# DoRA forward on one core: stores on ScalarE's ring, chunks in pairs, and part of block 0 loaded by GpSimd

## The chip, the core and the metric

The kernel runs on one core of a Trainium2 chip. The time is device microseconds of that core; the kernel before took 164.54 us, the median of 9 runs (164.23 to 164.89). A profiled execution gives the page and the trace that are read here.

## The reference

A weight matrix is adapted by a product of rank 16, its columns are normalised and scaled, and a batch of 32,768 rows of 256 numbers is multiplied by it.

```python
W_adapted = W + scale * (lora_A @ lora_B)                 # 256 x 256
W_norm = np.sqrt(np.sum(W_adapted ** 2, axis=0, keepdims=True) + 1e-8)
W_final = W_adapted / W_norm * m
y = x.reshape(-1, 256) @ W_final                          # 32768 x 256, float32
```

`x` and `y` have 33.55 MB each. All else is small: `W` has 256 KB.

## The kernel before

The rows of `x` are cut into 8 blocks (`NBLK`) of 4096 rows, 4 MB each. A block lies in SBUF as 128 partitions by 32 rows (`DJ`) of 256 numbers, so that a partition's share is 32 KB that follow each other in DRAM. There are five such buffers (`x_bufs`, L63). A block is worked on in 8 chunks (`CH`) of 4 rows per partition (`J`), 64 chunks in all.

SyncE issues all large transfers on one ring. It loads `W` and then the first five blocks (`load_x`, L106 to L121). After that its loop (L124 to L131) waits until block b is done, issues its store (L126), waits until the store of block b-1 has landed and issues the load of the block that takes that buffer. ScalarE's ring carries only the three small loads of `lora_A`, `lora_B` and `m` (L115 to L119).

The prologue makes the final weights in bf16 (`w_final`): four small products on TensorE (L213 to L229), the arithmetic on VectorE (L158 to L182) and the square root on ScalarE (L195).

After that each chunk goes through five engines. GpSimd waits for the block's load at its first chunk and rounds the chunk to bf16 (L151, `xb`, four buffers). TensorE turns it by four transposes of pairs of bf16 that are read as fp32 (`turned`, L243, into one of four PSUM tiles `xt_ps`). VectorE copies that tile to SBUF (L185, `xt`, four buffers). TensorE multiplies it with `w_final` in eight matmuls (`product`, L254, into one of two PSUM tiles `y_ps`). ScalarE copies the result over the chunk of `x` that it came from (L202), and after the eighth chunk of a block it drains and raises `done` (L206), for which SyncE waits.

The order on TensorE is written out by hand: a loop over the 8 blocks (L268), whose body turns chunk 0 and then, for each chunk, turns the next chunk of the same block before it multiplies this one. `take` (L234) waits for a semaphore and takes one from it, which makes the body the same in each round. `head_slot` places the head of the loop among the instructions. At the end of the program SyncE waits for the last five stores (L280).

Of the kernel before, what the change touches and what calls it, by code (L numbers as in the profile page):

```python
# [11 lines left out]
def kernel(  # L12
# [10 lines left out]
    nc = tc.nc  # L23
    P = 128
    FP32 = mybir.dt.float32
    BF16 = mybir.dt.bfloat16
# [3 lines left out]
    x_flat = x.flatten_outer_dims()  # L30
    out_flat = out.flatten_outer_dims()
    N, IN = x_flat.shape
    OUT = W.shape[1]
    R = lora_A.shape[1]
    KC = IN // P
    J = 4
    DJ = 32
    BLK = DJ * P
    NBLK = N // BLK
# [3 lines left out]
    XBUFS = 5  # L43
    CH = DJ // J
    NCH = NBLK * CH
    NXB = 4
    NXT = 4
    F4 = J * P

    PE = mybir.EngineType.PE  # L50

# [5 lines left out]
    def sb(name, shape, dtype):  # L57
        return ctx.enter_context(nc.sbuf_tensor(name, shape, dtype))

    def ps(name, shape, dtype):  # L60
        return ctx.enter_context(nc.psum_tensor(name, shape, dtype))

    x_bufs = [sb(f"x_sb{k}", [P, DJ, IN], FP32) for k in range(XBUFS)]  # L63
    xb_bufs = [sb(f"xb{k}", [P, J, IN], BF16) for k in range(NXB)]
    xt_bufs = [sb(f"xt{k}", [P, F4, KC], BF16) for k in range(NXT)]
    w_nat = sb("w_nat", [P, KC, OUT], FP32)
    a_nat = sb("a_nat", [P, KC, R], FP32)
    b_nat = sb("b_nat", [R, OUT], FP32)
# [13 lines left out]
    m_all = sb("m_all", [P, OUT], FP32)  # L82
    w_final = sb("w_final", [P, KC, OUT], BF16)

    xt_ps = [ps(f"xt_ps{k}", [P, F4], FP32) for k in range(4)]
    y_ps = [ps(f"y_ps{k}", [P, J, OUT], FP32) for k in range(2)]

    aT_ps = y_ps[0][0:R, 0, :]
# [2 lines left out]
    mb_ps = y_ps[1][:, 2, :]  # L91


    late = [nc.alloc_semaphore(f"store{b}") for b in range(NBLK - XBUFS, NBLK)]
    sems = {f"store{b}": late[b - NBLK + XBUFS] for b in range(NBLK - XBUFS, NBLK)}

    def sem(name):
        if name not in sems:
            sems[name] = tc.alloc_semaphore(name)
        return sems[name]  # L100

    def rows(dram, b):
        return dram[b * BLK : (b + 1) * BLK].rearrange("(p j) k -> p j k", p=P)


    def load_x(b):  # L106
        nc.sync.dma_start(out=x_bufs[b % XBUFS][:], in_=rows(x_flat, b)).then_inc(
            sem(f"load{b}"), 16
        )


    nc.sync.dma_start(
        out=w_nat[:], in_=W.rearrange("(p t) o -> p t o", t=KC)
    ).then_inc(sem("load_w"), 16)
    nc.scalar.dma_start(  # L115
        out=a_nat[:], in_=lora_A.rearrange("(p t) r -> p t r", t=KC)
    ).then_inc(sem("load_a"), 16)
    nc.scalar.dma_start(out=b_nat[:], in_=lora_B).then_inc(sem("load_b"), 16)
    nc.scalar.dma_start(out=m_row[:], in_=m[None, :]).then_inc(sem("load_m"), 16)  # L119
    for b in range(XBUFS):  # L120
        load_x(b)  # L121


    for b in range(NBLK):  # L124
        nc.sync.wait_ge(sem("done"), b + 1)
        nc.sync.dma_start(out=rows(out_flat, b), in_=x_bufs[b % XBUFS][:]).then_inc(  # L126
            sem(f"store{b}"), 16
        )
        if b >= 1 and b - 1 + XBUFS < NBLK:
            nc.sync.wait_ge(sem(f"store{b - 1}"), 16)  # L130
            load_x(b - 1 + XBUFS)  # L131


    nc.gpsimd.memset(zeros[:], 0.0).then_inc(sem("pool"), 1)
# [2 lines left out]
        out=identity[:],  # L137
        in_=zeros[:],
# [3 lines left out]
        pattern=[[-1, P]],  # L142
        channel_multiplier=1,
    ).then_inc(sem("ident"), 1)
    for g in range(NCH):
        b, c = divmod(g, CH)
        if c == 0:
            nc.gpsimd.wait_ge(sem(f"load{b}"), 16)
        if g >= NXB:
            nc.gpsimd.wait_ge(sem("turned"), g - NXB + 1)  # L150
        nc.gpsimd.tensor_copy(  # L151
            out=xb_bufs[g % NXB][:],
            in_=x_bufs[b % XBUFS][:, c * J : (c + 1) * J, :],
        ).then_inc(sem("rounded"), 1)


    dv = sem("dve")
# [9 lines left out]
        out=wa[:], in0=ab_ps, scalar=float(scale), in1=w_nat[:], op0=ALU.mult, op1=ALU.add  # L167
# [6 lines left out]
    for t in range(KC):  # L174
        i = nc.vector.tensor_mul(out=wam[:, t], in0=wa[:, t], in1=m_all[:])  # L175
# [4 lines left out]
    for t in range(KC):  # L180
        i = nc.vector.tensor_mul(out=w_final[:, t], in0=wam[:, t], in1=rnorm[:])  # L181
    i.then_inc(dv, 1)  # L182
    for g in range(NCH):
        nc.vector.wait_ge(sem("turned"), g + 1)
        nc.vector.tensor_copy(  # L185
            out=xt_bufs[g % NXT][:].rearrange("p r t -> p (r t)").bitcast(FP32),
            in_=xt_ps[g % 4][:],
        ).then_inc(sem("copied"), 1)


# [5 lines left out]
        out=norm[:], in_=n2_ps, func=AF.Sqrt, bias=eps_col[:]  # L196
    ).then_inc(sem("act"), 1)
    for g in range(NCH):
        b, c = divmod(g, CH)
        nc.scalar.wait_ge(sem("product"), g + 1)  # L200

        nc.scalar.copy(  # L202
            out=x_bufs[b % XBUFS][:, c * J : (c + 1) * J, :], in_=y_ps[g % 2][:]
        ).then_inc(sem("room"), 1)
        if c == CH - 1:
            nc.scalar.drain().then_inc(sem("done"), 1)  # L206


    pe = sem("pe")
# [2 lines left out]
    for t in range(KC):  # L212
        i = nc.tensor.transpose(aT_ps[:, t * P : (t + 1) * P], a_nat[:, t, :], identity[:])  # L213
    i.then_inc(pe, 1)
    nc.tensor.wait_ge(dv, 2)
    for t in range(KC):
        i = nc.tensor.matmul(  # L217
            ab_ps[:, t, :], aT[:, t * P : (t + 1) * P], b_bf[:], start=True, stop=True
        )
# [3 lines left out]
    for t in range(KC):  # L223
        i = nc.tensor.matmul(  # L224
            n2_ps, ones[:], sq[:, t, :], start=(t == 0), stop=(t == KC - 1)
        )
# [7 lines left out]
    def take(name):  # L234

        nc.tensor.sem_inc(sem(name), -1).wait_op(sem(name), 1, "sem-ge")  # L236

    j_order = []
# [1 line left out]
        j_order.append(a)  # L240
        j_order.append(a + J // 2)

    def turned(c):  # L243
        take("rounded")

        for j in range(J):
            i = nc.tensor.transpose(  # L247
                xt_ps[c % 4][:, j * P : (j + 1) * P],
                xb_bufs[c % NXB][:, j, :].bitcast(FP32),
                identity[:],  # L250
            )
        i.then_inc(sem("turned"), 1)

    def product(c):  # L254
        take("copied")
        take("room")
        for t in range(KC):
            for j in j_order:
                i = nc.tensor.matmul(  # L259
                    y_ps[c % 2][:, j, :],  # L260
                    xt_bufs[c % NXT][:, j * P : (j + 1) * P, t],
                    w_final[:, t, :],
                    start=(t == 0 and (j % (J // 2)) == 0),
                    stop=(t == KC - 1 and (j % (J // 2)) == (J // 2) - 1),
                )
        i.then_inc(sem("product"), 1)

    with nc.Fori(0, NBLK, 1, engines=[PE], head_slot={PE: 0}):  # L268
        turned(0)
        for c in range(CH):  # L270
            if c + 1 < CH:
                turned(c + 1)
            product(c)


    critical.close()
# [40 lines left out]
```

## Time and profile before

| what | value |
|---|---|
| median of 9 runs | 164.54 us (164.23 to 164.89) |
| profiled execution | 164.6 us |
| its span, first to last instruction | 163.3 us |
| busy: TensorE matmuls, ScalarE, GpSimd, VectorE | 100.1, 66.8, 65.4, 49.7 us |
| moved by DMA | 67.45 MB, 413 GB/s over the span |
| read and written in HBM | 33.85 and 33.55 MB |
| loads of `x`: 8 of 4 MB, median from issue to landing | 29.6 us |
| stores: 8 of 4 MB, median from issue to landing | 35.7 us |
| last ScalarE copy begins, last store is issued | 139.66 us, 140.74 us |

The span is counted from the first to the last instruction of the profiled execution; the run's own time is somewhat longer. The page cuts the span into 40 slices of 4.08 us and gives each engine's busy share of a slice in tenths; the row DMA is the mean over the 16 DMA engines. The table of queues gives packets, megabytes and the time of the packets as a share of the 16 engines' span[...]. The waits are ordered by who waited for whom, with the total, the number and the longest in us. The stretches give, between two times, the busy time of each engine with its number of instructions, the granted clock of TensorE, the DMA share and the rate.

### The profile page before, as it was taken

Reading aid. Unit: us, or ns where it says so; the run is one execution under the profiler, and the core shown is the slowest. Engines: PE = TensorE matmul, PEld = TensorE weight load, DVE = VectorE, ACT = ScalarE, POOL = GpSimd, SP = SyncE. Lnnn points to the kernel's source line nnn. Section 1 sums busy time; section 2 is a strip of 40 time slices with the busy share of each in tenths; the row PEclk is TensorE's granted clock in tenths of the full one; section 3 lists DMA queues with packets and bytes.
Section 4 is the critical chain, followed back from the end, with each engine's and each line's share of the span. In section 5 each row is a group of like instructions: output and inputs, shape, how many; then the busy total and the mean of one; then the engine's idle time right before and its main releaser. Section 6 shows DMA issues by size and latency. Waiting matters only on the chain. (4 is left out here: it accounts for less than half of the span.)

```text
span 163.3 us, 2077 instructions
## 1 busy us (share of the span) xinstructions
PE 100.1 (61%) x778; PEld 83.9 (51%) x778; DVE 49.7 (30%) x76; ACT 66.8 (41%) x67; POOL 65.4 (40%) x70
## 2 busy tenths in 40 slices
PE   1453999898998998991008993099921999200000
PEld 0212798796996996980006991079811788100000
DVE  0444453554454453550003450034500355000000
ACT  3010278577576775773000774007740257400000
POOL 1006938966876785500019800296004950000000
PEclk9999999999999999998555999759997599855555
DMA  5999998999999999999999999999999999999990
GB/s 201 434 458 393 453 441 385 490 409 425 458 401 337 425 393 468 425 393 482 401 449 441 401 468 425 395 458 425 425 449 409 458 433 401 458 425 425 449 409 40
DMA packets 2630, 67.45 MB, mean 413 GB/s; under 512 B 433, under 2 KB 450, under 8 KB 578
## 3 DMA queue, kind: packets, MB, share of 16 engines
q1 hardware_dynamic: 2448, 67.37, 96.7%
q10 hardware_dynamic: 178, 0.03, 0.1%
q8 instruction: 1, 0.02, 0.0%
q14 instruction: 3, 0.02, 0.0%
HBM read 33.85 MB, written 33.55 MB: 413 GB/s over the span
## 5 line engine op out<-in xcount | busy, mean ns | idle before, releaser
L202 ACT COPY x_sb<-y_ps 128x1024 f32<-128x1024 f32 x64 | 64.8, 1013 | 66.2 <-PE y_ps L259 66.2
L151 POOL CAST xb<-x_sb 128x1024 bf16<-128x1024 f32 x64 | 64.7, 1040 | 67.1 <-DMA x_sb<-in_x_dram 56.8
L259 PE MATMUL y_ps<-w_final,xt 128*128 128x256 bf16 x512 | 70.0, 282 | 3.8 <-PEq L236 3.6
L185 DVE COPY xt<-xt_ps 128x512 f32<-128x512 f32 x64 | 43.9, 691 | 80.4 <-PE xt_ps L247 80.4
L247 PE MATMUL xt_ps<-identity,xb 128*128 128x128 f32 x256 | 42.2, 297 | 29.9 <-PEq L236 29.9
L259 PEld LDWEIGHTS y_ps<-w_final,xt 128*128 128x128 bf16 x512 | 50.6, 101 | 14.6 <-issue 8.1
L247 PEld LDWEIGHTS xt_ps<-identity,xb 128*128 128x128 f32 x256 | 32.9, 154 | 33.2 <-issue 32.4
L224 PE MATMUL y_ps<-sq,ones 128*128 128x256 f32 x4 | 2.1, 674 | 1.6 <-DVE sq L170 1.6
L213 PE MATMUL y_ps<-identity,a_nat 128*16 128x128 f32 x2 | 0.6, 394 | 3.5 <-DMA a_nat<-in_lora_A_dram 3.5
L195 ACT ACTIVATE norm<-y_ps,eps_col 128x256 f32<-128x256 f32 x1 | 0.5, 473 | 5.3 <-PE y_ps L224 5.3
L224 PEld LDWEIGHTS y_ps<-sq,ones 128*128 128x128 f32 x4 | 1.2, 324 | 2.3 <-DVE sq L170 2.1
L193 ACT ACT_TABLE_LOAD x1 | 1.3, 1283 | 2.4 <-issue 2.4
L213 PEld LDWEIGHTS y_ps<-identity,a_nat 128*16 128x16 f32 x2 | 0.1, 88 | 3.5 <-issue 3.5
L178 DVE RECIPROCAL rnorm<-norm 128x256 f32<-128x256 f32 x1 | 1.7, 1747 | 0.0
L172 DVE COPY m_all<-y_ps 128x256 f32<-128x256 f32 x1 | 0.4, 424 | 3.3 <-PE y_ps L229 3.3
L229 PE MATMUL y_ps<-m_row,ones 1*128 1x256 f32 x2 | 1.2, 710 | 0.0
L161 DVE CAST b_bf<-b_nat 16x256 bf16<-16x256 f32 x1 | 0.3, 282 | 2.9 <-DMA b_nat<-in_lora_B_dram 2.9
L217 PE MATMUL y_ps<-b_bf,aT 16*128 16x256 bf16 x2 | 0.6, 404 | 0.7 <-DVE aT L163 0.7
L166 DVE SCALAR_TENSOR_TENSOR wa<-y_ps,w_nat 128x512 f32<-128x512 f32 x1 | 0.7, 691 | 0.8 <-PE y_ps L217 0.8
L229 PEld LDWEIGHTS y_ps<-m_row,ones 1*128 1x128 f32 x2 | 0.5, 308 | 0.7 <-issue 0.7
L175 DVE TENSOR_TENSOR wam<-wa,m_all 128x256 f32<-128x256 f32 x2 | 0.8, 422 | 0.0
L181 DVE TENSOR_TENSOR w_final<-wam,rnorm 128x256 bf16<-128x256 f32 x2 | 0.8, 421 | 0.0
(12 smaller groups left out, 2.5 us busy)
## 6 DMA issues: line engine op xcount, KB each, us to landing
x_sb<-in_x_dram SPq DMA_DIRECT2D x8, 4096.0 KB, 29.6
out_dram<-x_sb SPq DMA_DIRECT2D x8, 4096.0 KB, 35.7
w_nat<-in_W_dram SPq DMA_DIRECT2D x1, 256.0 KB, 2.9
a_nat<-in_lora_A_dram ACTq DMA_DIRECT2D x1, 16.0 KB, 2.5
b_nat<-in_lora_B_dram ACTq DMA_DIRECT2D x1, 16.0 KB, 2.8
m_row<-in_m_dram ACTq DMA_DIRECT2D x1, 1.0 KB
```

What stands on the lines that cost most here:

```text
L151: nc.gpsimd.tensor_copy(out=xb_bufs[g % NXB][:], in_=x_bufs[b % XBUFS][:, c * J : (c + 1) * J, :],).then_inc(sem("rounded"), 1)
L166: nc.vector.scalar_tensor_tensor(out=wa[:], in0=ab_ps, scalar=float(scale), in1=w_nat[:], op0=ALU.mult, op1=ALU.add).then_inc(dv, 1)
L175: i = nc.vector.tensor_mul(out=wam[:, t], in0=wa[:, t], in1=m_all[:])
L178: nc.vector.reciprocal(out=rnorm[:], in_=norm[:]).then_inc(dv, 1)
L181: i = nc.vector.tensor_mul(out=w_final[:, t], in0=wam[:, t], in1=rnorm[:])
L185: nc.vector.tensor_copy(out=xt_bufs[g % NXT][:].rearrange("p r t -> p (r t)").bitcast(FP32), in_=xt_ps[g % 4][:],).then_inc(sem("copied"), 1)
L193: nc.scalar.activation(out=warm[:], in_=eps_col[:], func=AF.Sqrt)
L202: nc.scalar.copy(out=x_bufs[b % XBUFS][:, c * J : (c + 1) * J, :], in_=y_ps[g % 2][:]).then_inc(sem("room"), 1)
L224: i = nc.tensor.matmul(n2_ps, ones[:], sq[:, t, :], start=(t == 0), stop=(t == KC - 1))
L229: nc.tensor.matmul(mb_ps, ones[0:1, :], m_row[:], start=True, stop=True).then_inc(pe, 1)
L247: i = nc.tensor.transpose(xt_ps[c % 4][:, j * P : (j + 1) * P], xb_bufs[c % NXB][:, j, :].bitcast(FP32), identity[:],)
L259: i = nc.tensor.matmul(y_ps[c % 2][:, j, :], xt_bufs[c % NXT][:, j * P : (j + 1) * P, t], w_final[:, t, :], start=(t == 0 and (j % (J // 2 ...
```

## The change

The change has two parts. In the first, SyncE's ring keeps only loads: each load of a buffer that was used before waits for the store from that buffer. ScalarE issues a block's store itself, right after its drain. The last block is loaded and stored in two halves (`parts` has nine entries). GpSimd rounds, TensorE turns and VectorE copies two chunks at a time, with two buffers of twice the size in place of four; the products and ScalarE's copies remain by chunk. TensorE's loop has 16 rounds of two pairs; the first pair is turned ahead of the loop, and each round turns the first pair of the next. For the last round GpSimd writes a pair of zeros, which is turned and not used. The head of the loop stands at slot 128.

In the second, the first 12 of the 32 rows per partition of block 0 are loaded by three DMAs of GpSimd, over 5, 120 and 3 partitions, in pieces of 4096 bytes. SyncE's first load has the other 20 rows. GpSimd waits for all four before its first cast.

```diff
--- before.py
+++ after.py
@@ -43,9 +43,17 @@
     XBUFS = 5
     CH = DJ // J
     NCH = NBLK * CH
-    NXB = 4
-    NXT = 4
-    F4 = J * P
+    NPR = NCH // 2
+    PRB = CH // 2
+    NXB = 2
+    EARLY = 12
+    SPARE = 4
+    SHARES = [(0, SPARE + 1), (SPARE + 1, 120), (SPARE + 121, 7 - SPARE)]
+    NXT = 2
+    F8 = 2 * J * P
     PE = mybir.EngineType.PE
@@ -61,8 +69,8 @@
         return ctx.enter_context(nc.psum_tensor(name, shape, dtype))
     x_bufs = [sb(f"x_sb{k}", [P, DJ, IN], FP32) for k in range(XBUFS)]
-    xb_bufs = [sb(f"xb{k}", [P, J, IN], BF16) for k in range(NXB)]
-    xt_bufs = [sb(f"xt{k}", [P, F4, KC], BF16) for k in range(NXT)]
+    xb_bufs = [sb(f"xb{k}", [P, 2 * J, IN], BF16) for k in range(NXB)]
+    xt_bufs = [sb(f"xt{k}", [P, F8, KC], BF16) for k in range(NXT)]
     w_nat = sb("w_nat", [P, KC, OUT], FP32)
     a_nat = sb("a_nat", [P, KC, R], FP32)
     b_nat = sb("b_nat", [R, OUT], FP32)
@@ -82,7 +90,7 @@
     m_all = sb("m_all", [P, OUT], FP32)
     w_final = sb("w_final", [P, KC, OUT], BF16)
-    xt_ps = [ps(f"xt_ps{k}", [P, F4], FP32) for k in range(4)]
+    xt_ps = [ps(f"xt_ps{k}", [P, F8], FP32) for k in range(2)]
     y_ps = [ps(f"y_ps{k}", [P, J, OUT], FP32) for k in range(2)]
     aT_ps = y_ps[0][0:R, 0, :]
@@ -91,22 +99,42 @@
     mb_ps = y_ps[1][:, 2, :]
-    late = [nc.alloc_semaphore(f"store{b}") for b in range(NBLK - XBUFS, NBLK)]
-    sems = {f"store{b}": late[b - NBLK + XBUFS] for b in range(NBLK - XBUFS, NBLK)}
+    late = [nc.alloc_semaphore(f"store{b}") for b in range(NBLK - XBUFS, NBLK + 1)]
+    sems = {f"store{NBLK - XBUFS + k}": s for k, s in enumerate(late)}
     def sem(name):
         if name not in sems:
             sems[name] = tc.alloc_semaphore(name)
         return sems[name]
-    def rows(dram, b):
-        return dram[b * BLK : (b + 1) * BLK].rearrange("(p j) k -> p j k", p=P)
-    def load_x(b):
-        nc.sync.dma_start(out=x_bufs[b % XBUFS][:], in_=rows(x_flat, b)).then_inc(
-            sem(f"load{b}"), 16
-        )
+    parts = [(b * CH, CH) for b in range(NBLK - 1)]
+    parts += [(NCH - CH, CH // 2), (NCH - CH // 2, CH // 2)]
+    part_of = {}
+    for n, (g0, cnt) in enumerate(parts):
+        for g in range(g0, g0 + cnt):
+            part_of[g] = n
+    def in_sbuf(g0, cnt):
+        b, c = divmod(g0, CH)
+        return x_bufs[b % XBUFS][:, c * J : (c + cnt) * J, :]
+    def in_dram(dram, g0, cnt):
+        return dram[g0 * J * P : (g0 + cnt) * J * P].rearrange("(p j) k -> p j k", p=P)
+    def load_x(n):
+        s = EARLY if n == 0 else 0
+        nc.sync.dma_start(
+            out=in_sbuf(*parts[n])[:, s:, :], in_=in_dram(x_flat, *parts[n])[:, s:, :]
+        ).then_inc(sem(f"load{n}"), 16)
+    def store_y(n):
+        nc.scalar.dma_start(
+            out=in_dram(out_flat, *parts[n]), in_=in_sbuf(*parts[n])
+        ).then_inc(sem(f"store{n}"), 16)
     nc.sync.dma_start(
@@ -117,18 +145,11 @@
     ).then_inc(sem("load_a"), 16)
     nc.scalar.dma_start(out=b_nat[:], in_=lora_B).then_inc(sem("load_b"), 16)
     nc.scalar.dma_start(out=m_row[:], in_=m[None, :]).then_inc(sem("load_m"), 16)
-    for b in range(XBUFS):
-        load_x(b)
-    for b in range(NBLK):
-        nc.sync.wait_ge(sem("done"), b + 1)
-        nc.sync.dma_start(out=rows(out_flat, b), in_=x_bufs[b % XBUFS][:]).then_inc(
-            sem(f"store{b}"), 16
-        )
-        if b >= 1 and b - 1 + XBUFS < NBLK:
-            nc.sync.wait_ge(sem(f"store{b - 1}"), 16)
-            load_x(b - 1 + XBUFS)
+    for n in range(len(parts)):
+        b = parts[n][0] // CH
+        if b >= XBUFS and parts[n][0] % CH == 0:
+            nc.sync.wait_ge(sem(f"store{b - XBUFS}"), 16)
+        load_x(n)
     nc.gpsimd.memset(zeros[:], 0.0).then_inc(sem("pool"), 1)
@@ -142,16 +163,27 @@
         pattern=[[-1, P]],
         channel_multiplier=1,
     ).then_inc(sem("ident"), 1)
-    for g in range(NCH):
-        b, c = divmod(g, CH)
-        if c == 0:
-            nc.gpsimd.wait_ge(sem(f"load{b}"), 16)
-        if g >= NXB:
-            nc.gpsimd.wait_ge(sem("turned"), g - NXB + 1)
+    for k, (p0, cnt) in enumerate(SHARES):
+        nc.gpsimd.dma_start(
+            out=in_sbuf(*parts[0])[p0 : p0 + cnt, 0:EARLY, :],
+            in_=in_dram(x_flat, *parts[0])[p0 : p0 + cnt, 0:EARLY, :],
+            max_dma_last_dim=4096,
+        ).then_inc(sem(f"early{k}"), 16)
+    for k in range(len(SHARES)):
+        nc.gpsimd.wait_ge(sem(f"early{k}"), 16)
+    for p in range(NPR):
+        b, c = divmod(p, PRB)
+        if p == 0 or part_of[2 * p - 1] != part_of[2 * p]:
+            nc.gpsimd.wait_ge(sem(f"load{part_of[2 * p]}"), 16)
+        if p >= NXB:
+            nc.gpsimd.wait_ge(sem("turned"), p - NXB + 1)
         nc.gpsimd.tensor_copy(
-            out=xb_bufs[g % NXB][:],
-            in_=x_bufs[b % XBUFS][:, c * J : (c + 1) * J, :],
+            out=xb_bufs[p % NXB][:],
+            in_=x_bufs[b % XBUFS][:, 2 * c * J : 2 * (c + 1) * J, :],
         ).then_inc(sem("rounded"), 1)
+    nc.gpsimd.wait_ge(sem("turned"), NPR - NXB + 1)
+    nc.gpsimd.memset(xb_bufs[NPR % NXB][:], 0.0).then_inc(sem("rounded"), 1)
     dv = sem("dve")
@@ -180,11 +212,11 @@
     for t in range(KC):
         i = nc.vector.tensor_mul(out=w_final[:, t], in0=wam[:, t], in1=rnorm[:])
     i.then_inc(dv, 1)
-    for g in range(NCH):
-        nc.vector.wait_ge(sem("turned"), g + 1)
+    for p in range(NPR):
+        nc.vector.wait_ge(sem("turned"), p + 1)
         nc.vector.tensor_copy(
-            out=xt_bufs[g % NXT][:].rearrange("p r t -> p (r t)").bitcast(FP32),
-            in_=xt_ps[g % 4][:],
+            out=xt_bufs[p % NXT][:].rearrange("p r t -> p (r t)").bitcast(FP32),
+            in_=xt_ps[p % 2][:],
         ).then_inc(sem("copied"), 1)
@@ -202,8 +234,11 @@
         nc.scalar.copy(
             out=x_bufs[b % XBUFS][:, c * J : (c + 1) * J, :], in_=y_ps[g % 2][:]
         ).then_inc(sem("room"), 1)
-        if c == CH - 1:
+        n = part_of[g]
+        if g == NCH - 1 or part_of[g + 1] != n:
             nc.scalar.drain().then_inc(sem("done"), 1)
+            nc.scalar.wait_ge(sem("done"), n + 1)
+            store_y(n)
     pe = sem("pe")
@@ -240,37 +275,39 @@
         j_order.append(a)
         j_order.append(a + J // 2)
-    def turned(c):
+    def turned(p):
         take("rounded")
-        for j in range(J):
+        for j in range(2 * J):
             i = nc.tensor.transpose(
-                xt_ps[c % 4][:, j * P : (j + 1) * P],
-                xb_bufs[c % NXB][:, j, :].bitcast(FP32),
+                xt_ps[p % 2][:, j * P : (j + 1) * P],
+                xb_bufs[p % NXB][:, j, :].bitcast(FP32),
                 identity[:],
             )
         i.then_inc(sem("turned"), 1)
-    def product(c):
+    def product(p):
         take("copied")
-        take("room")
-        for t in range(KC):
-            for j in j_order:
-                i = nc.tensor.matmul(
-                    y_ps[c % 2][:, j, :],
-                    xt_bufs[c % NXT][:, j * P : (j + 1) * P, t],
-                    w_final[:, t, :],
-                    start=(t == 0 and (j % (J // 2)) == 0),
-                    stop=(t == KC - 1 and (j % (J // 2)) == (J // 2) - 1),
-                )
-        i.then_inc(sem("product"), 1)
-    with nc.Fori(0, NBLK, 1, engines=[PE], head_slot={PE: 0}):
+        for h in range(2):
+            take("room")
+            for t in range(KC):
+                for j in j_order:
+                    r = (h * J + j) * P
+                    i = nc.tensor.matmul(
+                        y_ps[h][:, j, :],
+                        xt_bufs[p % NXT][:, r : r + P, t],
+                        w_final[:, t, :],
+                        start=(t == 0 and (j % (J // 2)) == 0),
+                        stop=(t == KC - 1 and (j % (J // 2)) == (J // 2) - 1),
+                    )
+            i.then_inc(sem("product"), 1)
+    turned(0)
+    with nc.Fori(0, NPR // 2, 1, engines=[PE], head_slot={PE: 128}):
+        turned(1)
+        product(0)
+        product(1)
         turned(0)
-        for c in range(CH):
-            if c + 1 < CH:
-                turned(c + 1)
-            product(c)
     critical.close()
```

## The prediction

> **What bounds the kernel now.** I read the page's slices and its DMA queues first, then the chain that ended last, then what SyncE's queue waited for, and last the busy time by stretches, which I chose so that the two ends and the crossings from loads to stores stand apart. The slices and queues of the page:
>
> ```profile
> span 163.3 us, 2077 instructions
> DMA  5999998999999999999999999999999999999990
> q1 hardware_dynamic: 2448, 67.37, 96.7%
> q8 instruction: 1, 0.02, 0.0%
> q14 instruction: 3, 0.02, 0.0%
> ```
>
> One ring, q1, carries 67.37 MB and keeps 16 DMA engines busy for 96.7% of 163.3 us, 157.9 us. That is 4.211 MB per engine, so 26.7 GB/s each: 1.23 us for a packet of 32 KB (a partition's row of one block), 0.46 us for 12 KB. The bytes are given by the problem, so this kernel is its DMA engines. The arithmetic is not the bound. Of the chain of instructions that ended last (start, length, what):
>
> ```profile
> 138.59 1.05 PE y_ps L259 x8
> 139.66 1.01 ACT x_sb L202
> ```
>
> and of what SyncE's queue waited for (total, times, longest):
>
> ```profile
> SPq L126 <- ACTq L206: 80.7, 5, 25.1
> SPq L107 <- DMA out_dram<-x_sb: 52.1, 3, 24.7
> SPq L281 <- DMA out_dram<-x_sb: 20.7, 3, 9.7
> ```
>
> The arithmetic ends at 140.7 us, and 22.6 us of stores follow. SyncE waits 80.7 and 52.1 us before stores and loads, and this costs nothing while its ring is full: the DMA row shows no empty slice in between. What is left to gain is 163.3 − 157.9 = 5.4 us: the start before the first packets (2.00 us, in which a stretch 0 to 2 has a DMA share of 0.03) and the end. By stretches (start:end, length, then five engines, clock, DMA share, GB/s):
>
> ```profile
> 47.00:54.00 7.00, 6.26 (x57) 5.44 (x55) 2.77 (x5) 4.47 (x5) 4.58 (x5) 1.00 0.95 337
> 98.00:106.00 8.00, 1.28 (x11) 0.71 (x8) 0.10 (x1) 2.02 (x2) 0.97 (x1) 0.88 0.97 415
> 118.00:124.00 6.00, 1.48 (x13) 0.86 (x10) 0.30 (x1) 2.21 (x3) 0.00 (x0) 1.00 1.00 426
> 126.00:158.00 32.00, 13.43 (x96) 10.93 (x95) 5.53 (x8) 8.10 (x8) 6.64 (x7) 0.66 0.99 429
> 158.00:159.00 1.00, 0.00 (x0) 0.00 (x0) 0.00 (x0) 0.00 (x0) 0.00 (x0) 0.50 1.14 492
> 159.00:162.00 3.00, 0.00 (x0) 0.00 (x0) 0.00 (x0) 0.00 (x0) 0.00 (x0) 0.50 0.15 66
> 162.00:163.30 1.30, 0.00 (x0) 0.00 (x0) 0.00 (x0) 0.00 (x0) 0.00 (x0) 0.50 0.00 0
> ```
>
> A packet counts in the stretch in which it starts. From 159 to 162 the share is 0.15 of 16 engines, 2.4, and 66 GB/s is 2.5 engines at 26.7: about two of sixteen engines still have packets, while the other fourteen began their last one before 159.0 and were through by 159.0 + 1.2 = 160.2 us. **Two late engines, 3 us late**, set the end: every store needs all sixteen. Levelled, their 2 × 3.0 us would lie on 16 engines, 0.4 us each: a span of 160.6, a gain of 2.7 us.
>
> [...]
>
> **The change part by part.** The sum is made against the profiled execution, which took 164.6 us, its span and 1.3 us around it; the median, 164.54, is 0.06 below.
>
> *Early rows.* 12 of 32 rows of block 0 move from SyncE's ring to GpSimd's in shares of 5, 120 and 3 partitions, 12 KB each. [...] No bytes are added: −2.7 us at most, if the other late engine is cured as well; nothing if it isn't. The three issues on GpSimd are not in the trace; between 0.35 us each (a store's issue on SyncE took 332 to 451 ns) and a few us they stand in time in which GpSimd waits 12.2 us for block 0.
>
> *TensorE's loop of half a block, turned a pair ahead; rounding and copying in pairs.* GpSimd's 64 casts of 1.04 us become 32 of about 2.1, VectorE's 64 copies of 0.69 become 32 of about 1.3; TensorE's 70.0 and 42.2 us of matmuls are the same work plus one turn of zeros at the end (8 matmuls of 0.3, after the last product). Two buffers of a pair hold what four of a chunk did. Cost: 0, hidden by DMA; TensorE sits idle through whole slices. If that cover went, a pair instead of a chunk costs one more cast, 1 us, per load. What the edit can give is fewer fetches: half the body of the loop, half the casts and copies. The trace's fetches are one of 16 KB, 0.6 us, and 24 KB, 0.9 us, together at most 1.5 us on one engine, half of the second engine's lateness. Zero to 1.5; the remainder is unknown, so I take it that the second engine keeps 0.4 us beyond the levelled end, and let the rival have the case that it keeps it all.
>
> *Stores on ScalarE's ring.* Nine issues of 0.35 us, 3 us in all, with a drain and a wait, come onto ScalarE, behind which its next copies queue, and TensorE for `room`. ScalarE is busy 66.8 of 163.3 us: 0. SyncE's loads no longer stand behind `done`. What changes is the order on the DMA engines: now loads and stores go out in turns. From about 30 or 45 us, when the first store comes, to about 125, where the loads end, each engine alternates. Nearest rows: the crossings. 98 to 106 had 415 GB/s against 429, 3% less; 118 to 124 had 426, 1% less. If turns cost as crossings do: 0 to 3% of 95 us, 0 to 2.9 us. The first crossing is dearer: 337 GB/s over 7 us, 1.5 us lost. It may be gone with a mixed order, so the lower end is −1.5. I take +0.3, a tenth of the dear end, as one of the two later crossings lost next to nothing.
>
> *Last block in halves.* Its arithmetic can begin half a load, about 5 us, sooner and its last store is half as long. Before, stores alone fill 22.6 us after the arithmetic. With turns the loads still end some 30 us before the end, eight chunks need about 12 us, so there is cover: 0; one more store and load add 16 semaphore writes each, under 0.1 us.
>
> Sum: 160.6 levelled, 0.4 that stays with a late engine, 0.3 for turns: 161.3. With 1.3 around it 162.6, and 0.06 less against the median: **162.5 us**.
>
> **The rivals.** *One late engine stays* (the spared one isn't a late one, or the second isn't cured): 163.3 + 0.2 + 0 to 0.3 + 1.3 = 164.8 to 165.1; 164.6 if it is an engine to which the shares add nothing. For it: the trace has two late engines, one is relieved, and it doesn't say which they are. This is also the rival that the change doesn't do what it says.
> *Turns cost as crossings do*: 160.6 + 0.4 + 2.9 + 1.3 = 165.2, slower. For it 415 GB/s; against it 426 in the other crossing.
> *The early rows come late*, on the slower side. If the rings are served packet by packet, a 4 KB packet of GpSimd's gets a turn for each packet of 20 or 32 KB of SyncE's. 24 early packets per engine then wait for 8 × 0.77 + 16 × 1.23 us and land at about 3 + 6 + 20 + 4 = 33 us, where block 0 is now there at 13.9. The first store follows 15.2 us after the first cast (29.1 against 13.9), at 48; the five loads last to about 52. So it is hidden, by 4 us. At two of SyncE's packets per turn all five loads pass first: landing at 52, first store at 67, and the DMA engines dry for 15 us: 162.5 + 15 = 177.5. The point is a landing later than 52 − 15 = 37 us.
> *The first crossing's loss goes*: 162.5 − 1.5 = 161.0.
>
> **How the numbers follow.** Both late engines cut: 0.54. First loss gone besides: 0.06. One stays late: 0.19, of which 0.11 within 0.2% and 0.08 slower. Turns dear: 0.14. Early rows late: 0.07. 0.2% is 0.33 us, about what a measurement of this kernel tells from no change. Faster 0.60, same 0.11, slower 0.29. The range leaves out the late rows and the upper part of the dear turns: 161.0 to 165.6. The likeliest case by itself spans 161.6 to 163.6.
>
> **What would show it.** Right: after the last full stretch the DMA share falls to nothing within 1.5 us; the instruction queues have fewer packets; GpSimd's first cast starts before 37 us; full stretches with both rings keep 425 GB/s or more. Wrong: a stretch of 3 us with a share of 0.06 to 0.15 at the end (a late engine), 415 GB/s in the mixed stretches (dear turns), an empty slice near 52 us (late rows).

## The result, and the profile after

The changed kernel takes 185.73 us, the median of 10 runs (184.86 to 186.96), against 164.50 (163.98 to 164.89): a ratio of 1.129, 95% interval 1.127 to 1.131. The profiled execution took 185.63 us with a span of 184.3. Times below are medians of all executions and ratios compare fast ones only, since two were slow: 174.64 us of the larger pieces in three shares, and 169.94 us of the stores' ring alone, the one with the profile, so that the trace read for that ring is a repeat's.

The page's slices, queues (packets, MB, share of 16 engines) and one DMA issue (KB, us to landing):

```profile
span 184.3 us, 1993 instructions
...
DMA  6998999999996007969899999999999999999993
...
q1 hardware_dynamic: 1440, 32.24, 45.2%
q10 hardware_dynamic: 1474, 33.59, 42.5%
q0 software_dynamic: 528, 1.57, 2.4%
q14 instruction: 2, 0.02, 0.0%
...
x_sb<-in_x_dram POOLq DMA_DIRECT2D x1, 1440.0 KB, 44.7
```

Two things stand out. The DMA row has two empty slices in the middle, where before it had none. And 1.57 MB on GpSimd's queue took 44.7 us to land, in which sixteen engines at the 429 GB/s of before move twelve times as much. Who waited for it, in the waits (total, times, longest), and in GpSimd's order of time (start, length):

```profile
POOL xb L180 <- DMA x_sb<-in_x_dram: 63.1, 3, 48.1
```

```profile
52.22 3.72 POOL L180 CAST xb<-x_sb 128x2048 bf16<-128x2048 f32 x2 [48.09 <-DMA x_sb<-in_x_dram]
```

The first cast starts at 52.22 us; it was 13.88. Before, GpSimd's first casts, and SyncE's first two stores:

```profile
13.88 7.92 POOL L151 CAST xb<-x_sb 128x1024 bf16<-128x1024 f32 x8 [12.21 <-DMA x_sb<-in_x_dram]
29.08 11.88 SPq L126 DMA_DIRECT2D out_dram<-x_sb  x2
```

After, the first stores follow the casts, in ScalarE's order of time:

```profile
70.02 0.37 ACTq L135 DMA_DIRECT2D out_dram<-x_sb  x1
83.24 0.37 ACTq L135 DMA_DIRECT2D out_dram<-x_sb  x1
```

The five loads need nothing from the arithmetic and end near 60 us. Then the DMA engines have nothing to do until 70. By stretches (start:end, length, five engines, clock, DMA share, GB/s):

```profile
4.00:53.00 49.00, 4.41 (x10) 1.91 (x10) 5.61 (x10) 0.47 (x1) 0.91 (x2) 1.00 1.02 376
53.00:61.00 8.00, 6.43 (x39) 5.51 (x40) 2.45 (x2) 1.85 (x2) 6.68 (x4) 1.00 0.66 283
61.00:71.00 10.00, 8.61 (x76) 7.25 (x73) 3.58 (x4) 5.86 (x7) 4.93 (x3) 1.00 0.10 43
71.00:80.00 9.00, 7.51 (x64) 6.19 (x64) 3.49 (x4) 4.87 (x6) 6.06 (x4) 1.00 0.98 419
80.00:86.00 6.00, 5.18 (x46) 4.57 (x47) 2.35 (x2) 3.25 (x4) 3.19 (x3) 1.00 0.79 262
86.00:94.00 8.00, 6.67 (x58) 5.45 (x57) 2.36 (x2) 5.25 (x6) 4.50 (x3) 1.00 0.93 377
94.00:150.00 56.00, 47.87 (x412) 40.18 (x409) 19.73 (x17) 32.89 (x35) 29.88 (x16) 1.00 1.00 428
```

Each stretch's loss against the 429 GB/s of before is its length times the missing share of the rate: 49 × (1 − 376/429) = 6.1 us while the early rows are under way, 2.7 + 9.0 us until the first store, 0.2, then 2.3 us in which for the most part the second store isn't ready and only a load or nothing is under way, and 1.0 us after it. Together 21.3 us; the span grew by 21.0. The kernel before didn't have its full rate all the time either: from 4 to 94 us it moved 425 GB/s and the changed one 327, which is 90 × (1 − 327/425) = 20.8 us. So nearly the whole of it lies before 94 us. In the first stretch the DMA share is 1.02 while the rate is 376: the engines are busy and slow, which an idle share would not have shown. From 12 to 44 us, before and then after:

```profile
12.00:44.00 32.00, 27.41 (x228) 23.94 (x229) 15.09 (x23) 17.87 (x18) 23.21 (x24) 1.00 1.00 432
12.00:44.00 32.00, 0.00 (x0) 0.00 (x0) 3.40 (x6) 0.00 (x0) 0.00 (x0) 1.00 1.01 361
```

### The profile page after: what moved, and what is told of

Its sections match the earlier page's. It is cut to its first block, busy times and chain, and to the rows that moved or that the text cites. A ratio compares the mean times of both kernels' runs of the same rounds, so it can differ in the third digit from the quotient of the medians.

```text
span 184.3 us, 1993 instructions
## 1 busy us (share of the span) xinstructions
PE 98.9 (54%) x786; PEld 81.1 (44%) x786; DVE 43.7 (24%) x44; ACT 63.6 (35%) x67; POOL 64.4 (35%) x42
## 3 DMA queue, kind: packets, MB, share of 16 engines
q0 software_dynamic: 528, 1.57, 2.4%
## 5 line engine op out<-in xcount | busy, mean ns | idle before, releaser
L234 ACT COPY x_sb<-y_ps 128x1024 f32<-128x1024 f32 x64 | 61.7, 1014 | 96.5 <-PE y_ps L296 96.5
L180 POOL CAST xb<-x_sb 128x2048 bf16<-128x2048 f32 x32 | 59.8, 1896 | 98.2 <-DMA x_sb<-in_x_dram 63.1
L296 PE MATMUL y_ps<-w_final,xt 128*128 128x256 bf16 x512 | 62.0, 273 | 14.8 <-PEq L271 14.8
L217 DVE COPY xt<-xt_ps 128x1024 f32<-128x1024 f32 x32 | 37.9, 1221 | 112.1 <-PE xt_ps L282 112.1
L282 PE MATMUL xt_ps<-identity,xb 128*128 128x128 f32 x264 | 35.3, 291 | 48.1 <-PEq L271 48.1
L296 PEld LDWEIGHTS y_ps<-w_final,xt 128*128 128x128 bf16 x512 | 47.1, 98 | 29.0 <-issue 21.8
L282 PEld LDWEIGHTS xt_ps<-identity,xb 128*128 128x128 f32 x264 | 32.1, 151 | 49.7 <-issue 49.5
L167 POOL DMA_DIRECT2D x_sb<-in_x_dram x3 | 2.1, 705 | 0.3 <-issue 0.3
L186 POOL MEMSET xb<- 128x2048 bf16 x1 | 1.8, 1805 | 0.3 <-PE xt_ps L282 0.3
## 6 DMA issues: line engine op xcount, KB each, us to landing
x_sb<-in_x_dram POOLq DMA_DIRECT2D x1, 1440.0 KB, 44.7
```

The source lines that it names most:

```text
L167: nc.gpsimd.dma_start(out=in_sbuf(*parts[0])[p0 : p0 + cnt, 0:EARLY, :], in_=in_dram(x_flat, *parts[0])[p0 : p0 + cnt, 0:EARLY, :], max_dm ...
L180: nc.gpsimd.tensor_copy(out=xb_bufs[p % NXB][:], in_=x_bufs[b % XBUFS][:, 2 * c * J : 2 * (c + 1) * J, :],).then_inc(sem("rounded"), 1)
L186: nc.gpsimd.memset(xb_bufs[NPR % NXB][:], 0.0).then_inc(sem("rounded"), 1)
L217: nc.vector.tensor_copy(out=xt_bufs[p % NXT][:].rearrange("p r t -> p (r t)").bitcast(FP32), in_=xt_ps[p % 2][:],).then_inc(sem("copied"), 1)
L234: nc.scalar.copy(out=x_bufs[b % XBUFS][:, c * J : (c + 1) * J, :], in_=y_ps[g % 2][:]).then_inc(sem("room"), 1)
L282: i = nc.tensor.transpose(xt_ps[p % 2][:, j * P : (j + 1) * P], xb_bufs[p % NXB][:, j, :].bitcast(FP32), identity[:],)
```

## The experiments

Theory A: the early rows get one turn of 4 KB for each packet of 32 KB, come late, and the DMA engines run dry. Theory B: the rest of the change costs the time. Theory C: GpSimd's DMAs are slow of themselves. Theory D came after the first four runs: the shape of the shares.

**The second part left out** (`EARLY = 0`, without GpSimd's DMAs and their waits).

> The changed kernel without its second part: block 0 comes whole by SyncE's ring, GpSimd issues no DMA. Theory A (the early rows get one turn of 4 KB for each packet of 32 KB, land at about 50 us, and the DMA engines run dry until the first store at 70 us): first cast at 14 us, first store at about 29 us, no empty slice, 161.5 to 165 us. Theory B (the loss is in the rest: pairs that make a block's arithmetic take 13.2 us where it took 11.9, loads that wait for stores on another ring): the loss stays, 178 us or more.

163.93 us, ratio 0.998 (0.997 to 0.999). First cast at 13.90 us, first store at 32.33, no empty slice. Theory B falls. Loads and stores in turns, from 75 to 120 us:

```profile
75.00:120.00 45.00, 31.15 (x228) 25.43 (x227) 10.84 (x9) 18.07 (x19) 17.70 (x10) 0.85 1.00 431
159.00:160.00 1.00, 0.00 (x0) 0.00 (x0) 0.00 (x0) 0.00 (x0) 0.00 (x0) 0.50 0.16 66
160.00:162.00 2.00, 0.00 (x0) 0.00 (x0) 0.00 (x0) 0.00 (x0) 0.00 (x0) 0.50 0.06 25
```

431 GB/s: turns between two rings of full packets cost nothing here. At the end a share of 0.06, one engine of sixteen, works on alone until 162.

**The second part alone** on the kernel before. These are its issues; `...` stands for GpSimd's three waits and SyncE's load of the other 20 rows.

```diff
+    for k, (p0, cnt) in enumerate(SHARES):        # 5, 120, 3
+        nc.gpsimd.dma_start(
+            out=x_bufs[0][p0 : p0 + cnt, 0:EARLY, :],
+            in_=rows(x_flat, 0)[p0 : p0 + cnt, 0:EARLY, :],
+            max_dma_last_dim=4096,
+        ).then_inc(sem(f"early{k}"), 16)
...
```

> The kernel before with only the early rows added: 12 of 32 rows of block 0 by GpSimd in shares of 5, 120 and 3 partitions and pieces of 4 KB, stores still on SyncE's ring, chunks alone. Theory A: first cast at about 50 us, first store at about 65, dry engines between 58 and 65, 175 to 184 us. Theory B: 164 to 167 us.

185.03 us, ratio 1.126 (1.123 to 1.130), a little above theory A's range. The first cast comes at 54.32 us, and nine microseconds have no packet at all:

```profile
4.00:53.00 49.00, 4.00 (x9) 1.80 (x8) 5.60 (x10) 0.47 (x1) 0.13 (x1) 1.00 1.01 356
61.00:70.00 9.00, 8.61 (x78) 7.60 (x76) 4.11 (x8) 7.09 (x7) 6.20 (x7) 1.00 0.00 0
```

The early rows alone make a loss of this size.

**Larger pieces.**

```diff
-            max_dma_last_dim=4096,
+            max_dma_last_dim=12288,
```

> The changed kernel with the early rows in pieces of 12 KB, a third as many. Theory A: 8 turns in place of 24, so they land at 10 + 8 x 1.9 = 25 us, first store at about 43 us, no dry stretch, 162 to 166 us. Theory C (GpSimd's DMAs are slow of themselves, whatever the pieces and whatever runs beside them): landing at 45 us or later, 178 us or more.

172.07 us, ratio 1.046 (1.044 to 1.048); first cast at 34.12 us. Both theories miss. Fewer pieces help, but the cast came 24 us after most pieces began, at about 10 us, where 8 turns at the full rate would take 8 × 1.67 = 13. The packets' own times in the trace say why: from 10 to 30 us a piece of 12 KB took 0.75 us in the middle (at the full rate 0.46), and a packet of 32 KB beside it 1.90 us (before: 1.21). That is 2.65 us a turn and 21 us for 8, with the last share behind them. The rate in that stretch:

```profile
10.00:30.00 20.00, 0.61 (x2) 0.00 (x0) 3.61 (x6) 0.00 (x0) 0.00 (x0) 1.00 1.01 284
```

**Loads of later blocks held back** until the early rows have landed.

```diff
+        if n == 1:
+            for k in range(len(SHARES)):
+                nc.sync.wait_ge(sem(f"early{k}"), 16)
         load_x(n)
```

> The changed kernel with SyncE's load of block 1 issued only after the early rows have landed, so that pieces of 4 KB compete with block 0 alone. Theory A: they land at 14 to 17 us, the ring stands empty for about 2 us there, first store at about 31 us, 163 to 167 us. Theory C: they land after 30 us and the loads behind them come later still, 185 us or more.

171.18 us, ratio 1.043 (1.041 to 1.045); first cast at 18.72 us. Outside both again. With nothing beside them, the pieces have no turn to wait for, and still:

```profile
11.00:17.00 6.00, 0.00 (x0) 0.00 (x0) 3.27 (x6) 0.00 (x0) 0.00 (x0) 1.00 0.87 194
```

194 GB/s, a little under half of 429, with pieces of 4 KB that took 0.31 us in the middle, where 0.16 is the full rate (a run below). What remains is GpSimd's ring itself, theory C, or the shape of its DMAs, the large one over 120 partitions and not 128: theory D. How a shape would slow the transfer is in no trace; theory D is a supposition, and the next runs try it.

**One share of 128 partitions**, with pieces of 4 KB and of 12 KB.

```diff
-    SHARES = [(0, SPARE + 1), (SPARE + 1, 120), (SPARE + 121, 7 - SPARE)]
+    SHARES = [(0, 128)]
```

> The changed kernel with the early rows in one DMA of 128 partitions in place of 5, 120 and 3; pieces of 4 KB as before, so 24 per DMA engine. Theory A (turns alone): as with three shares, 24 turns of 1.63 us each, landing at about 49 us, packets of 32 KB beside them still 1.43 to 1.48 us, 361 GB/s, 184 us. Theory D (the shape: [...]): packets of 32 KB take 1.21 us again and pieces 0.16, 430 GB/s, a turn 1.37, landing at about 43 us, first store at 61, 174 to 177 us.

> The changed kernel with the early rows in one DMA of 128 partitions and in pieces of 12 KB, 8 per DMA engine. With three shares such pieces took 0.75 us and the packets of 32 KB beside them 1.9, 284 GB/s, cast at 34.1 us, 172.1 us. Theory D: pieces take 0.46 and packets 1.21 us, 430 GB/s; landing at 10 + 8 x 1.67 = 24 us, first store at 43, before the loads end at 53: 163.5 to 165 us. Theory C (GpSimd's DMAs are slow of themselves): still 0.75 and 1.9 us, 172 us.

With 4 KB: 169.34 us, ratio 1.030 (1.029 to 1.032), below the range. The packets' times are theory D's: 0.159 us for a piece in the middle, 1.213 us for a packet of 32 KB. The cast came at 36.28 us, sooner than I wrote, because the pieces began sooner: 60 of the 384 had begun by 10 us, among block 0's own packets, and 90 by 10.8, where I had the first begin at 10 and the changed kernel has 18 by then. From 10.8 to 34.6 us, when the last one ended, there are 294 pieces and 275 packets of 32 KB, so about one piece to a packet, as supposed. Why they begin sooner than in three shares was not found. The engines still run dry for a short time, and up to 84 us there are too few stores to fill them:

```profile
12.00:34.00 22.00, 0.05 (x1) 0.00 (x0) 3.61 (x6) 0.00 (x0) 0.00 (x0) 1.00 1.00 427
34.00:53.00 19.00, 13.36 (x93) 11.07 (x94) 4.80 (x4) 6.16 (x7) 11.18 (x6) 1.00 0.94 404
53.00:56.00 3.00, 2.31 (x22) 2.07 (x20) 1.59 (x2) 1.55 (x2) 1.56 (x1) 1.00 0.41 175
56.00:66.00 10.00, 8.67 (x75) 7.13 (x75) 3.12 (x3) 5.95 (x7) 5.90 (x4) 1.00 0.86 367
66.00:84.00 18.00, 15.26 (x134) 13.03 (x132) 7.07 (x6) 9.99 (x11) 10.59 (x6) 1.00 0.96 377
```

By the count used above, 1.8 us are lost from 53 to 56 and 1.4 + 2.2 us from 56 to 84.

With 12 KB: 163.55 us, ratio 0.996 (0.995 to 0.997), within theory D's range. Pieces take 0.460 us, packets 1.213. Here too the pieces began sooner, 48 of 128 by 10 us: landing at about 18 us where I had 24, first store at 37.35:

```profile
10.00:22.00 12.00, 1.52 (x8) 1.42 (x8) 3.61 (x6) 0.00 (x0) 3.42 (x2) 1.00 1.05 454
22.00:53.00 31.00, 27.08 (x214) 22.32 (x213) 11.87 (x10) 15.67 (x17) 17.90 (x11) 1.00 1.00 415
```

Theory C falls: with a whole share GpSimd's ring keeps the full rate here. Whether this version still relieves an engine was not shown.

**The shape without GpSimd**: SyncE issues the early rows ahead of the rest, in shares of 120 and 8, then of 112 and 16; `...` stands for GpSimd's issues, which go.

```diff
+        if n == 0:
+            for k, (p0, cnt) in enumerate(SHARES):    # (0, 120), (120, 8)
+                nc.sync.dma_start(
+                    out=in_sbuf(*parts[0])[p0 : p0 + cnt, 0:EARLY, :],
+                    in_=in_dram(x_flat, *parts[0])[p0 : p0 + cnt, 0:EARLY, :],
+                ).then_inc(sem(f"early{k}"), 16)
...
```

> The changed kernel with the early rows issued by SyncE, ahead of the other 20 rows, in shares of 120 and 8 partitions; GpSimd issues no DMA, so there are no turns between its ring and SyncE's. [...] Theory D: the pieces of 12 KB take 0.75 to 0.9 us here too, the early rows 3 to 4 us longer than at the full rate, first cast at about 17.5 us where it was 13.9 without early rows, and no dry stretch: 164 to 167 us[...]. Theory C: pieces of 0.46 us, cast at 14 us, 161.5 to 164.3 us.

> As the run in which SyncE issued the early rows in shares of 120 and 8 partitions (pieces of 12 KB took 0.91 us, first cast at 19.4 us, 168.45 us), with shares of 112 and 16. [...] Theory D1[...]: pieces of the large share take 0.46 to 0.6 us, first cast at 15 to 17 us, 164.5 to 166.5 us. Theory D2 (any share that isn't 128 partitions is slow): pieces of 0.9 us as with 120, cast at 19 us, 168 us.

With 120: 168.45 us, ratio 1.026 (1.025 to 1.028), first cast at 19.36. With 112: 165.49 us, ratio 1.005 (1.004 to 1.007), cast at 16.36. The middle piece of 12 KB took 0.91 us with 120, twice the full 0.46, and 0.62 with 112, about the upper end of theory D1. The stretch of the early rows with 120, and then with 112:

```profile
3.20:8.00 4.80, 0.58 (x2) 0.12 (x2) 0.03 (x1) 0.69 (x2) 0.00 (x0) 1.00 1.01 237
```

```profile
3.20:8.00 4.80, 2.10 (x6) 1.07 (x7) 2.00 (x4) 0.66 (x2) 0.00 (x0) 1.00 1.17 350
```

The rates are 0.55 and 0.82 of 429 GB/s. So the slowness belongs to the shape and not to a ring, and 112 partitions lose less than 120. With 120 the time is above its range; the next stretch, 8 to 12 us, in which the shares overlap the 20 rows behind them, had no more than 192 GB/s, by the same count 2.2 us. What in the shape slows the transfer was not shown: no run separates its two sides, SBUF and DRAM.

**TensorE's loop alone, the stores' ring alone, and both**, on the kernel before. For the ring, SyncE's loop of stores goes and ScalarE issues a block's store after its drain, as in the changed kernel. For the loop (`...` stands for the chunk of zeros of the last turn):

```diff
-    with nc.Fori(0, NBLK, 1, engines=[PE], head_slot={PE: 0}):
-        turned(0)
-        for c in range(CH):
-            if c + 1 < CH:
-                turned(c + 1)
-            product(c)
+    turned(0)
+    with nc.Fori(0, 2 * NBLK, 1, engines=[PE], head_slot={PE: 128}):
+        for c in range(CH // 2):
+            turned(c + 1)
+            product(c)
...
```

> The kernel before with TensorE's loop alone changed: half a block per round, the next chunk turned ahead across rounds, head at slot 128, one chunk of zeros at the end; chunks alone, stores on SyncE's ring. If this took the second late DMA engine away in the changed kernel: no packet of 16 KB on q8, one engine in place of two in the last 3 us (a share of 0.06 to 0.08 where it was 0.15), 163.9 to 164.3 us. If not: two late engines, 164.2 us.

> The kernel before with one edit: stores issued by ScalarE on its ring, loads on SyncE's; chunks, TensorE's loop, and the whole last block as before. If turns between loads and stores cost nothing, 430 GB/s in the mixed stretches. If TensorE's loop is what took the second late DMA engine away (the changed kernel without early rows has one, 2.9 us late, and no packet of queue q8), two late engines and the packet of q8 are here: 164 to 164.6 us. If the ring did that, one late engine, 163.5 to 164.

> The kernel before with stores on ScalarE's ring alone, once more, for its trace: 163.5 us; two late engines and the packet of q8 if the ring doesn't cure them, one if it does.

> Both edits together: stores on ScalarE's ring and TensorE's loop of half a block, with chunks alone, the last block whole and no early rows. If the two add up, 163.0 to 163.5 us, with one late engine; if the one late engine that stays sets the end whatever the rest does, 163.5 to 163.9 us, as each edit alone.

The loop alone: 165.29 us, ratio 1.004 (1.002 to 1.005), slower by 0.4% and above both of its cases. The queue q8 is gone and so is one late engine, but the other is later than before, about 4 us behind the rest:

```profile
159.00:160.00 1.00, 0.00 (x0) 0.00 (x0) 0.00 (x0) 0.00 (x0) 0.00 (x0) 0.50 0.08 33
160.00:161.00 1.00, 0.00 (x0) 0.00 (x0) 0.00 (x0) 0.00 (x0) 0.00 (x0) 0.50 0.08 33
161.00:163.00 2.00, 0.00 (x0) 0.00 (x0) 0.00 (x0) 0.00 (x0) 0.00 (x0) 0.50 0.08 33
```

The ring alone: 163.53 us, ratio 0.996 (0.995 to 0.997); in the repeat, a single execution of 164.01 us, q8's packet is there and so are two late engines: of the sixteen increments by which the last store's semaphore rises in the trace, fourteen come by 160.32 us and two at 162.21 and 162.67. So the ring cures none, though its time is what I had for one late engine. Both: 163.33 us, ratio 0.992 (0.991 to 0.993), in the range foreseen for edits that add up, and the fastest kernel of this study, ahead of both the kernel before and the changed one. The ratios of the two alone would make 1.000, though: the loop costs 0.4% on the kernel before and gives about 0.4% with the ring. In the profiled executions the one late engine's last increment comes 4.2 us behind the middle one without the ring and 2.4 us with it. Why was not found.

## Why the prediction was wrong

**What bounds it.** Right. Full stretches after the early rows run at 428 GB/s with two rings (94 to 150 us), as they ran before with one (429, from 126 to 158 us).

**Early rows: "−2.7 us at most … nothing if it isn't".** This step failed, and with it the forecast. I priced the relief and the issues (0.7 us each on GpSimd, as it turned out), and costed the transfer of 1.57 MB in this shape at nothing, since no bytes are added. The runs show two prices. The shape takes the DMA to 194 GB/s when alone and 361 beside full packets (12 to 44 us of the changed kernel; 432 before). And a landing at 52 us empties the ring. Making the share whole takes 185.73 to 169.34 us; making the pieces larger as well takes that to 163.55. These steps are 16.4 and 5.8 us; in the other order they are 13.7 and 8.5, so each makes the other dearer.

**The rival "early rows come late", 7 in 100, 177.5 us.** The right mechanism in the right place, with its terms too small and its chance far too low. With one packet to a turn it had the rows land at 33 us, hidden. I had the pieces begin beside block 0's own packets and a turn cost 1.38 us. On most engines they began at about 10 us, after those packets, and a turn cost 1.63 us: 10 + 24 × 1.63 = 49, with the last share behind, 52. That 52 us also stood in the prediction is luck: it came from two of SyncE's packets to a turn, and the trace has one (from 12 to 44 us, 320 pieces and 313 packets), but a slow one. The point from which it decides I put at 37 us. A cast at 36.28 us already ran dry for 1.8 us between 53 and 56 (a share of 0.41): the first store came 18.4 us after the cast, where it had been 15.2, and I had left the pairs out of that term.

**Relief of one engine.** An engine was relieved, but not the late one. That the shares spare one engine, and add 0.2 us to the others, was my estimate, which no trace of before showed. In the run with pieces of 12 KB and three shares, the sixteen increments of the last store's semaphore, in us about their middle:

```
-2.80 -0.60 -0.42 -0.37 -0.29 -0.17 -0.16 -0.05 0.05 0.17 0.25 0.44 1.21 1.58 1.64 3.12
```

One engine ends 2.8 us ahead, as much as six pieces of 12 KB at 0.46 us, and another is 3.1 us late as ever. In the changed kernel itself the relief is gone. At the fifth load one engine is still 2.0 us ahead (57.41 where the middle one is 59.39); then the engines run dry, and the sixteen increments of the first store come within 80.99 to 81.34 us, all level. By the last store none is more than 0.3 us ahead of the middle one, and one is again 2.9 us late, at 184.29. So the lateness is not left over from the start; an engine falls behind anew. The last one trails:

```profile
182.00:184.30 2.30, 0.00 (x0) 0.00 (x0) 0.00 (x0) 0.00 (x0) 0.00 (x0) 0.50 0.03 14
```

The rival with one late engine had this, and named that the trace doesn't say which engine is late; I gave it too little weight. Which one is late, and why, was not found.

**Loop and fetches: "zero to 1.5".** Half right. The fetches are the packets on the queues that the page calls instruction: one on q8 and three on q14 before, two on q14 in the changed kernel. The packet of q8 goes and with it one late engine, in the run without early rows and in that of the loop alone. It gives nothing by itself: a store's semaphore takes sixteen increments and is waited for until the last, and one late engine remains. The packet on q8, 16 KB, took 0.96 us, not 0.6, and that is still a third of the 3 us; that it makes the engine late is argued from the runs with and without it.

**Pairs: "0, hidden by DMA".** Right where there is cover: 163.93 us with pairs. The blocks follow each other every 13.22 us (70.02 to 83.24) where it was 11.55 (ScalarE's eighth copies, 28.00 and 39.55 us), and with the cover gone this shows: the second store comes 13.2 us after the first, and 80 to 86 us has 262 GB/s. Its price here was not measured apart: with chunks in the place of pairs and the early rows late, 185.03 us, but there the cast came 2.1 us later (54.32) and the first store at the same time (70.00), so by this estimate pairs cost about 2 us up to the first store.

**Stores' ring: +0.3.** The price was too high, if anything: 431 GB/s in turns, and the ring alone gains 0.4%. The rival "turns cost as crossings do" falls. Turns they are: from 108 to 126 us of the changed kernel 128 packets of loads and 112 of stores started. No run has the halves of the last block apart; a load or store adds sixteen packets of 4 bytes, as many as its semaphore's increments, of 9 ns each in the middle (272 for the 17 DMAs on q1 before).

**The sum.** 162.5 supposed that both late engines are cured. Without the early rows one is, and 163.93 was measured; what a cure of the other would give was not measured, as no run relieved it.

## What to carry to other kernels

When part of a saturated transfer is moved to another ring, price its shape before its bytes: shares of 120 and of 112 partitions ran at 0.55 and 0.82 of the full rate here, and with one of 128 the DMA kept 427 GB/s (pieces of 4 KB, 12 to 34 us). Take 128 whole partitions unless a run shows that another split keeps the rate. A small piece beside large packets waited for about one large packet each (320 pieces and 313 packets from 12 to 44 us of the changed kernel), so what the pipeline needs first must not come in small pieces on a second ring behind a full first one. And a DMA-bound kernel hides slow arithmetic only while the ring has other work, here the first five loads: work out by when the first store must be issued.

## What the runs showed that I had not expected

- A piece of 12 KB takes 0.46 us in a DMA of 128 partitions (on GpSimd's ring, beside SyncE's), 0.62 in one of 112 and 0.91 in one of 120 (both on SyncE's ring).
- The damage reaches the other ring: packets of 32 KB took 1.47 us in the middle beside pieces of 4 KB in shares of 5, 120 and 3, and 1.90 us beside pieces of 12 KB, against 1.21 with a whole share. The DMA share stood at 1.01 to 1.02 all the while.
- Without the packet on q8 one late engine is gone, and yet the kernel before became 0.4% slower with TensorE's new loop: in that trace the other one ends about 4 us behind.
